# Down products of a two-layer trunk: weight remainders subtracted on the vector engine, results alternating between two PSUM rings

## The chip, the cores and the metric

The kernel runs on one core of one Trainium2 chip. The metric is the device time of one execution, in microseconds (us). The profile names the engines PE (matrix products), PEld (their weight loads), DVE (vector engine), ACT (scalar engine), POOL (general-purpose engine, here above all an issuer of DMAs) and SP (the queue that issues most loads). Each engine takes its own instructions strictly in order.

## The reference

Two layers work on 128 context tokens and 512 latent tokens of width 1024, 640 columns in all:

```python
def ffn_sublayer(x, mod, k, g, w_in, w_out):
    h = modulated_norm(x, mod, k, g)
    gt, up = jnp.split(h @ w_in, 2, axis=-1)
    return x + 0.5 * mod[:, None, 3 * k + 2] * ((jax.nn.silu(gt) * up) @ w_out)

def trunk_layer(...):
    x = ffn_sublayer(x, mod, 0, norm_g[0], w_ffn_in[0], w_ffn_out[0])
    ...
    x = ffn_sublayer(x, mod, 2, norm_g[2], w_ffn_in[1], w_ffn_out[1])
```

Between the two sublayers stands a mixer of attention, pooling and convolution heads. The change concerns the second product of each of the four feed-forward sublayers (FFNs), `@ w_out`, with 2816 inner rows and 1024 outputs. I call it the down product.

## The kernel before

**Split products.** Every float32 product is made of three products of shorter numbers (`mm3`, L352 to L354): high weights by high data, high weights by low data, low weights by high data. So each weight tile that a DMA brings into a `raw` buffer becomes a high part `wh` (a rounding copy on ACT, L170) and a low part `wl`, which is raw minus `wh`. `split_w` has two ways to make `wl`. With an engine given, that engine subtracts (L176). Without one, ACT writes `-wh` into `wl` (L173), and POOL issues a DMA that adds `raw` onto it (L174). Buffers: `raw` 5, `wh` 4, `wl` 4 tiles of 128x1024. All stages share them: the weights of the up products (`w_ffn_in`), of the down products (`w_ffn_out`), and the tiles of the modulation product (`w_ada`, loaded at L150).

**Down product.** The 22 inner tiles of 128 rows come in five chunks (`FF_CHUNKS`: 5, 5, 4, 4, 4). After the up products of a chunk, `down(ch)` runs over the eight output tiles `x0` to `x7` and, for each, over two halves of 320 columns, which I call h0 and h1. One half takes 15 products (12 with four inner tiles) into one PSUM bank of the ring `acc` (4 banks). Then `update_x` (L518) on DVE adds the bank times the gate onto `x`: in two pieces of 128 and 192 columns for h0, in one of 320 for h1. Only then is the bank free. A weight tile is 128x640 and serves one output tile in chunks 0 and 1; it is 128x1024 and serves two in chunks 2 to 4. The last chunk goes through `last_product`, with all four weight tiles made beforehand.

**What lies around it.** In FFN 1 (layer 0, first) the up products are plain, and DVE also computes a modulation product from `w_ada` tiles (L309, L311). In the other three FFNs the up products from j = 3 on use a scheme with fewer products: `fast_weights` needs sums of weight blocks on DVE (L646) and splits of them (L176). There `fast_ends` of the last j is put off until the next j, so two `acc` banks (`a` and `c`) and one `wh`/`wl` tile stay taken during a down product. A second ring `mis` (3 banks) serves the modulation product on PE (L275), transposes and norms. In FFNs 2 and 3 a running modulation step holds one of its banks for several j.

**Order.** A scheduler puts each engine's instructions in order when the program is built; it also decides which buffer a tile takes and which semaphores a load waits for. So the loads, sums and splits of the next j stand among the updates of a down product.

Of the kernel before, what the change touches and what calls it, by code (L numbers as in the profile page):

```python
# [17 lines left out]
P = 128  # L18
# [78 lines left out]
def trunk_kernel(ctx: ExitStack, tc: tile.TileContext, i: dict, o: dict):  # L97
    nc = tc.nc
# [12 lines left out]
    def acc():  # L111
        return acc_p.tile([P, 512], F32, tag="acc", name="acc")

    def mis():
        return mis_p.tile([P, 512], F32, tag="mis", name="mis")
# [4 lines left out]
    def f32(ap):  # L120
        return ap.bitcast(F32)
# [14 lines left out]
    for b in range(T // P):  # L136
        s = slot(name="xin", shape=(D,))
        src = i["x_prompt"][0] if b == 0 else i["x_sample"][0, (b - 1) * P : b * P, :]
# [19 lines left out]
    def raw_w(loads, nk=KD, width=P, raw=None):  # L158

        raw = (raw or raw_tile())[:, : nk * width].rearrange("p (k c) -> p k c", k=nk)  # L160
        loads(raw)
        return raw, nk, width

    def split_w(raw, nk, width, eng=None):

        view = lambda t: t[:, : nk * width].rearrange("p (k c) -> p k c", k=nk)
        size, tag = (1024, "") if nk * width > 512 else (512, "s")
        h = view(whp.tile([P, size], F32R, tag="wh" + tag, name="wh", bufs=4 if tag == "" else 2))
        lo = view(wlp.tile([P, size], F32R, tag="wl" + tag, name="wl", bufs=4 if tag == "" else 2))
        nc.scalar.activation(h, raw, AF.Copy)  # L170
        if eng is None:

            nc.scalar.activation(lo, f32(h), AF.Copy, scale=-1.0)  # L173
            nc.gpsimd.dma_start(lo, raw, accum_op=ALU.add)  # L174
        else:
            eng.tensor_tensor(lo, raw, f32(h), op=ALU.subtract)  # L176
        return h, lo

    def load_raw(src, c0, width=P, raw=None):
        return raw_w(  # L180
            lambda raw: nc.sync.dma_start(raw, src[:, c0 : c0 + width].rearrange("(k p) c -> p k c", p=P)),
            src.shape[0] // P,
            width,
            raw,
        )
# [1 line left out]
    def load_w(loads, nk=KD, width=P):  # L187
        return split_w(*raw_w(loads, nk, width))

    def load_cols(src, c0, width=P):  # L190
        return split_w(*load_raw(src, c0, width))

    def load_rows(n, *loads):

# [31 lines left out]
    ps = mis()  # L226
# [124 lines left out]
    def mm3(out, wh, wl, xh, xl, start, stop, onto=False):  # L351
        nc.tensor.matmul(out, wh, xh, start=start, stop=False, skip_group_check=onto)  # L352
        nc.tensor.matmul(out, wh, xl, start=False, stop=False, skip_group_check=onto)  # L353
        return nc.tensor.matmul(out, wl, xh, start=False, stop=stop, skip_group_check=onto)  # L354
# [160 lines left out]
    def update_x(l, n, t, hf, ps):  # L515
        a = HALVES[hf][0]
        for s, e, j in SEGS[hf]:
            nc.vector.scalar_tensor_tensor(  # L518
                xT[t][:, s:e],
                ps[:, s - a : e - a],  # L520
                gates[l][n][:, t, j : j + 1],
                xT[t][:, s:e],
                op0=ALU.mult,
                op1=ALU.add,
            )

    def last_product(ws, rhs, l, n, finish, nxt):

        for hf, (a, b) in enumerate(HALVES):
            for t in range(KD):  # L530
                wh, wl = ws[t // 2]
                c = slice(t % 2 * P, t % 2 * P + P)
                ps = acc()
                for k in range(4):
                    mm3(
                        ps[:, :HALF],
                        wh[:, k, c],
                        wl[:, k, c],
                        rhs[k][:, 0, a:b],
                        rhs[k][:, 1, a:b],  # L540
                        k == 0,
                        k == 3,
                    )
                update_x(l, n, t, hf, ps)
                finish(t, hf)
                nxt(hf, t)
                yield
# [8 lines left out]
    def ffn(l, f, n, hs, side, finish, nxt, first=None):  # L556
        w_in = i["w_ffn_in"][l, f]
        w_out = i["w_ffn_out"][l, f]
        gs = {}

        def weights(j, s):
            return load_cols(w_in, s * DFF + j * P)
# [55 lines left out]
        def down(ch):  # L618
            j0, j1 = FF_CHUNKS[ch]
            nj = j1 - j0  # L620
            wide = 2 if nj <= 4 else 1
            for t0 in range(0, KD, wide):
                wh, wl = load_cols(w_out[j0 * P : j1 * P, :], t0 * P, wide * P)
                for t in range(t0, t0 + wide):
                    c = slice((t - t0) * P, (t - t0 + 1) * P)
                    for hf, (a, b) in enumerate(HALVES):
                        ps = acc()
                        for j in range(nj):
                            mm3(
                                ps[:, :HALF],  # L630
                                wh[:, j, c],
                                wl[:, j, c],
                                gs[j0 + j][:, 0, a:b],
                                gs[j0 + j][:, 1, a:b],
                                j == 0,
                                j == nj - 1,
                            )
                        update_x(l, n, t, hf, ps)
# [76 lines left out]
        for j in range(2, NJ):  # L715
            if first or j < PLAIN:
                up(j)
            else:
                ends = fast_ups(j, ends)
            side(j)  # L720
            if ch < len(FF_CHUNKS) - 2 and j == FF_CHUNKS[ch][1] + (2 if first else 1):
                down(ch)
                ch += 1
        ends()
        down(ch)
        j0, j1 = FF_CHUNKS[-1]
        ws = [load_cols(w_out[j0 * P : j1 * P, :], m * 256, 256) for m in range(4)]
        for _ in last_product(ws, [gs[j] for j in range(j0, j1)], l, n, finish, nxt):
            pass

# [605 lines left out]
    for x, (l, n) in enumerate(steps):  # L1336
        last = x == len(steps) - 1
        fast = not last and steps[x + 1][1] != 1
        new = Seven() if fast else Plain()
        if last:  # L1340
            nxt = output
        else:
            heads = []

            def nxt(hf, t):
                if t < KD - 1:
                    return
                heads.append(norm_head(hf))
                if hf == 1 and fast:
                    seven(*steps[x + 1], new, heads)  # L1350
                elif hf == 1:
                    for h in range(2):
                        norm_tail(*steps[x + 1], h, new, heads[h])

        finish = nothing if last else squares
        if n == 1:
            mixer(l, hs, finish, nxt)
        else:
            ffn(l, n // 2, n, hs, spread(budget.get((l, n), 0), 1 if x else 4, x == 0), finish, nxt, None if x else first_tiles)
        hs = new  # L1360
# [30 lines left out]
```

## Time and profile before

| | |
|---|---|
| median of 3 runs | 2430.79 us (2415.92 to 2435.45) |
| profiled execution | 2416.3 us, its span 2414.5 us |
| busy share: PE, DVE, ACT, POOL | 96%, 59%, 47%, 9% |
| mean granted PE clock | 0.985 of full |

The span runs from the first to the last instruction. A PE product of 320 columns is recorded with about 0.31 us, but a new one starts every 0.15 us, since they overlap; so the busy share says little, and idle stretches and the granted clock say more. "Idle before" is time in which an engine had nothing running, with what ended it.

### The profile page before, as it was taken

The page shows a single profiled execution, that of the slowest core. Times are in us where ns is not written, and L with a number is a line of the kernel's source. Part 1 is how long each engine was busy: PE and PEld are TensorE (multiplying, and loading weights), DVE is VectorE, ACT ScalarE, POOL GpSimd, SP SyncE. Part 2 cuts the span into 40 slices and gives each one's busy share as a digit, 9 for nine tenths or more (in the row PEclk, how much of TensorE's full clock was granted, in tenths as well). Part 3 has the DMA queues.
Part 4 walks back from the last instruction along what each step waited for, and adds up shares of the span by engine and source line. Part 5 has one row for each costly group of instructions (what it writes and reads, how often), then busy time and mean ns, then how long its engine had stood idle before and what let it go on. Part 6 is the DMA issues. An engine that isn't in the chain of part 4 may idle for free.

```text
span 2414.5 us, 41180 instructions
## 1 busy us (share of the span) xinstructions
PE 2319.0 (96%) x16594; PEld 2234.9 (93%) x16594; DVE 1424.6 (59%) x3021; ACT 1146.1 (47%) x1964; POOL 221.0 (9%) x269
## 2 busy tenths in 40 slices
PE   7899999999999999999999999999999989999999
PEld 6899999999978999999999999999898789999999
DVE  5546564456867646456577364574657675546563
ACT  4433333345667434343465353444566674344451
POOL 2111111111200010100000101001111000000000
PEclk9999999999999999999999999999999999999999
DMA  8879798867633564664654545536474243543433
GB/s 268 217 167 252 189 252 197 213 133 149 140 71 95 142 157 140 159 182 123 166 140 120 134 117 147 156 108 163 107 159 112 53 97 85 130 97 99 121 100 94
DMA packets 372119, 347.22 MB, mean 144 GB/s; under 512 B 29176, under 2 KB 304984, under 8 KB 371928
## 3 DMA queue, kind: packets, MB, share of 16 engines
q1 hardware_dynamic: 340932, 244.88, 33.9%
q0 software_dynamic: 30816, 99.63, 22.7%
q8 instruction: 131, 2.15, 0.4%
q14 instruction: 60, 0.49, 0.1%
q10 hardware_dynamic: 180, 0.07, 0.0%
HBM read 242.04 MB, written 2.88 MB: 101 GB/s over the span
## 4 chain that ended last, share of the span: by engine, by line
PE 70%; issue 12%; DMA 10%; DVE 5%; ACT 2%; POOL 1%; POOLq 0%; ACTq 0%; SPq 0%; DVEq 0%
PE acc L352 21%; PE acc L353 20%; PE acc L354 20%; DMA wl<-raw 5%; DMA raw<-in_w_ffn_in 4%; PE mis L275 2%; PE po L352 1%; PE po L353 1%; PE po L354 1%; POOL wl L174 1%; DMA raw<-in_w_ada 1%; PE acc L1060 1%; PE mis L1111 1%; PE po L1100 1%; DVE sums L646 1%
## 5 line engine op out<-in xcount | busy, mean ns | idle before, releaser
L352 PE MATMUL acc<-h,wh 128*128 128x320 f32 (+1 forms) x2808 | 879.6, 315 | 27.6 <-DVE x L518 6.3
L354 PE MATMUL acc<-h,wl 128*128 128x320 f32 (+1 forms) x2808 | 870.9, 311 | 10.1 <-DMA wl<-raw 10.1
L353 PE MATMUL acc<-h,wh 128*128 128x320 f32 (+1 forms) x2808 | 873.5, 312 | 4.5 <-DVE h L412 3.9
L170 ACT ACTIVATE wh<-raw 128x1024 fp32r<-128x1024 f32 (+2 forms) x332 | 305.7, 924 | 641.2 <-PE acc L353 462.3
L352 PEld LDWEIGHTS acc<-h,wh 128*128 128x128 f32 x2808 | 531.7, 190 | 44.0 <-issue 8.0
L354 PEld LDWEIGHTS acc<-h,wl 128*128 128x128 f32 x2808 | 531.8, 190 | 13.1 <-DMA wl<-raw 12.9
L353 PEld LDWEIGHTS acc<-h,wh 128*128 128x128 f32 x2808 | 532.4, 190 | 6.7 <-DVE h L412 4.1
L352 PE MATMUL acc<-g,wh 128*128 128x320 f32 x1408 | 442.8, 314 | 29.2 <-DVE x L518 29.2
L353 PE MATMUL acc<-g,wh 128*128 128x320 f32 x1408 | 441.2, 313 | 0.0
L354 PE MATMUL acc<-g,wl 128*128 128x320 f32 x1408 | 440.3, 313 | 0.2 <-DMA wl<-raw 0.2
L174 POOL DMA_DIRECT2D wl<-raw x214 | 186.6, 872 | 2072.5 <-ACT wl L173 1409.5
L518 DVE SCALAR_TENSOR_TENSOR x<-acc,gate,x 128x128 f32<-128x128 f32 (+2 forms) x480 | 195.5, 436 | 265.3 <-PE acc L354 264.0
L352 PEld LDWEIGHTS acc<-g,wh 128*128 128x128 f32 x1408 | 269.6, 191 | 33.3 <-DVE x L518 25.8
L354 PEld LDWEIGHTS acc<-g,wl 128*128 128x128 f32 x1408 | 269.3, 191 | 0.7 <-DMA wl<-raw 0.4
L353 PEld LDWEIGHTS acc<-g,wh 128*128 128x128 f32 x1408 | 269.5, 191 | 0.3
L170 ACT ACTIVATE wh<-sums 128x1024 fp32r<-128x1024 f32 x114 | 120.5, 1059 | 203.1 <-PE acc L353 169.9
L173 ACT ACTIVATE wl<-wh 128x1024 fp32r<-128x1024 f32 (+1 forms) x214 | 205.5, 961 | 3.5
L176 DVE TENSOR_TENSOR wl<-sums,wh 128x1024 fp32r<-128x1024 f32 x114 | 139.5, 1225 | 74.0 <-ACT wh L170 54.5
L311 DVE SCALAR_TENSOR_TENSOR sums<-raw,c,sums 128x512 f32<-128x512 f32 x196 | 134.5, 746 | 37.8 <-DMA raw<-in_w_ada 37.8
L646 DVE TENSOR_TENSOR sums<-raw 128x512 f32<-128x512 f32 x114 | 74.8, 688 | 85.0 <-DMA raw<-in_w_ffn_in 84.3
L176 DVE TENSOR_TENSOR wl<-raw,wh 128x1024 fp32r<-128x1024 f32 (+1 forms) x116 | 110.9, 958 | 15.2 <-ACT wh L170 13.8
L671 ACT ACTIVATE part<-acc 128x320 f32<-128x320 f32 x171 | 73.2, 428 | 36.7 <-PE acc L354 35.1
(201 smaller groups left out, 2527.8 us busy)
## 6 DMA issues: line engine op xcount, KB each, us to landing
raw<-in_w_ffn_in SPq DMA_DIRECT2D x176, 512.0 KB, 4.2
wl<-raw POOLq DMA_DIRECT2D x150, 512.0 KB, 5.5
raw<-in_w_ada SPq DMA_DIRECT2D x128, 512.0 KB, 4.8
raw<-in_w_ffn_out SPq DMA_DIRECT2D x48, 512.0 KB, 4.8
raw<-in_w_ffn_out SPq DMA_DIRECT2D x64, 320.0 KB, 3.7
wl<-raw POOLq DMA_DIRECT2D x64, 320.0 KB, 4.4
raw<-in_w_in SPq DMA_DIRECT2D x20, 512.0 KB, 5.7
adaw<-in_w_ada SPq DMA_DIRECT2D x16, 512.0 KB, 10.6
```

Of the source, the lines that this page charges most:

```text
L170: nc.scalar.activation(h, raw, AF.Copy)
L173: nc.scalar.activation(lo, f32(h), AF.Copy, scale=-1.0)
L174: nc.gpsimd.dma_start(lo, raw, accum_op=ALU.add)
L176: eng.tensor_tensor(lo, raw, f32(h), op=ALU.subtract)
L275: last = nc.tensor.matmul(ps[32 * g : 32 * g + 32, 0:P], c2[:, 2 * q + k, :], r[:, k, g * P : (g + 1) * P], start=(q + k == 0), stop=(q + ...
L311: nc.vector.scalar_tensor_tensor(part[:, j, :], r[:, k, :], c, part[:, j, :], op0=ALU.mult, op1=ALU.add)
L352: nc.tensor.matmul(out, wh, xh, start=start, stop=False, skip_group_check=onto)
L353: nc.tensor.matmul(out, wh, xl, start=False, stop=False, skip_group_check=onto)
L354: return nc.tensor.matmul(out, wl, xh, start=False, stop=stop, skip_group_check=onto)
L518: nc.vector.scalar_tensor_tensor(xT[t][:, s:e], ps[:, s - a : e - a], gates[l][n][:, t, j : j + 1], xT[t][:, s:e], op0=ALU.mult, op1=ALU.add,)
L646: add = lambda out, x, y: nc.vector.tensor_tensor(out, x, y, op=ALU.add)
L671: nc.scalar.activation(t, ps[:, :HALF], AF.Copy)
```

## The change

Two edits, both in the down products. The weights of all down products, `last_product`'s too, now get their low part by subtraction on DVE, where ACT's negated copy and POOL's adding DMA did it before. And in `down` the bank of h1 comes from `mis`, that of h0 from `acc` as before. `last_product` keeps `acc` for both halves.

```diff
-    def load_cols(src, c0, width=P):
-        return split_w(*load_raw(src, c0, width))
+    def load_cols(src, c0, width=P, eng=None):
+        return split_w(*load_raw(src, c0, width), eng)
...
             for t0 in range(0, KD, wide):
-                wh, wl = load_cols(w_out[j0 * P : j1 * P, :], t0 * P, wide * P)
+                wh, wl = load_cols(w_out[j0 * P : j1 * P, :], t0 * P, wide * P, nc.vector)
                 for t in range(t0, t0 + wide):
                     c = slice((t - t0) * P, (t - t0 + 1) * P)
                     for hf, (a, b) in enumerate(HALVES):
-                        ps = acc()
+                        ps = (acc, mis)[hf]()
...
-        ws = [load_cols(w_out[j0 * P : j1 * P, :], m * 256, 256) for m in range(4)]
+        ws = [load_cols(w_out[j0 * P : j1 * P, :], m * 256, 256, nc.vector) for m in range(4)]
```

PE's products keep their order, but for one small one of 128 columns; they only write other banks. What moves is seen at the first down product of FFN 2. SP's queue there, before: the loads of down weights 3 to 7 (`in_w_ffn_out`), then those of the next j (`in_w_ffn_in`), with the semaphores that each waits for. DMASW stands for DMAs that POOL issued, DMAHW for those of SP.

```order
L181 DMA raw_9226<-in_w_ffn_out 128x5x128 [waits DMAHW4_49,DMASW0_49,Activation_49]
L181 DMA raw_9268<-in_w_ffn_out 128x5x128 [waits DMAHW2_49,PE_49]
L181 DMA raw_9310<-in_w_ffn_out 128x5x128 [waits DMAHW5_49,DMASW1_49,Activation_49]
L181 DMA raw_9394<-in_w_ffn_out 128x5x128 [waits DMAHW6_49,DMASW2_49,Activation_49]
L181 DMA raw_9436<-in_w_ffn_in 128x8x128 [waits DMAHW7_49,DMASW3_49,Activation_49]
L181 DMA raw_9438<-in_w_ffn_in 128x8x128 [waits DMAHW0_49,DMASW4_49,Activation_49]
```

The same loads now:

```order
L181 DMA raw_9195<-in_w_ffn_out 128x5x128 [waits DMAHW4_49,DVE_49]
L181 DMA raw_9236<-in_w_ffn_out 128x5x128 [waits DMAHW5_49,DVE_49]
L181 DMA raw_9277<-in_w_ffn_out 128x5x128 [waits DMAHW2_49,PE_49]
L181 DMA raw_9359<-in_w_ffn_out 128x5x128 [waits DMAHW6_49,DVE_49]
L181 DMA raw_9400<-in_w_ffn_in 128x8x128 [waits DMAHW7_49,DVE_49]
L181 DMA raw_9402<-in_w_ffn_in 128x8x128 [waits DMAHW0_49,DVE_49]
```

The loads stand in the same order; those that waited for the landing of an adding DMA now wait for DVE. The pair of `in_w_ffn_in` waited for the adding DMAs of down weights 3 and 4, and now waits for their subtractions.

DVE's queue at the updates of `x2` and `x3` of that down product, before:

```order
L518 SCALAR_TENSOR_TENSOR x2_94<-acc_9209,gate02_4741,x2_94 128x320
L518 SCALAR_TENSOR_TENSOR x3_95<-acc_9233,gate02_4741,x3_95 128x128
L518 SCALAR_TENSOR_TENSOR x3_95<-acc_9233,gate02_4741,x3_95 128x192
L646 TENSOR_TENSOR sums_9440<-raw_9436,raw_9438 128x512
L646 TENSOR_TENSOR sums_9440<-raw_9438 128x512
L176 TENSOR_TENSOR wl_9451<-raw_9438,wh_9450 128x512
L518 SCALAR_TENSOR_TENSOR x3_95<-acc_9251,gate02_4741,x3_95 128x320
```

And now, from the subtraction of down weight 4 on:

```order
L176 TENSOR_TENSOR wl_9239<-raw_9236,wh_9238 128x640
L518 SCALAR_TENSOR_TENSOR x2_94<-acc_9160,gate02_4721,x2_94 128x128
L518 SCALAR_TENSOR_TENSOR x2_94<-acc_9160,gate02_4721,x2_94 128x192
L518 SCALAR_TENSOR_TENSOR x2_94<-mis_9178,gate02_4721,x2_94 128x320
L646 TENSOR_TENSOR sums_9404<-raw_9400,raw_9402 128x512
L176 TENSOR_TENSOR wl_9280<-raw_9277,wh_9279 128x640
L646 TENSOR_TENSOR sums_9404<-raw_9402 128x512
L518 SCALAR_TENSOR_TENSOR x3_95<-acc_9201,gate02_4721,x3_95 128x128
L518 SCALAR_TENSOR_TENSOR x3_95<-acc_9201,gate02_4721,x3_95 128x192
```

The subtractions of the down weights stand among the updates. The first sum of the next j, which reads the pair of `in_w_ffn_in`, has moved up by one half: from behind h0 of `x3` to behind h1 of `x2`, ahead of the subtraction of down weight 5 (`wl_9280`). The same move is found in five more down products of FFNs 2 to 4, those of chunks 0 and 1; in chunk 2 the sums stand around the updates of `x0` in both kernels.

## Rows read from the trace of the kernel before

**Rows 1.** The page's first part: engine, busy us (share), instructions.

```profile
PE 2319.0 (96%) x16594; PEld 2234.9 (93%) x16594; DVE 1424.6 (59%) x3021; ACT 1146.1 (47%) x1964; POOL 221.0 (9%) x269
```

**Rows 2.** The view of waits: waiting line, releaser, total us, times, longest.

```profile
PE acc L352 <- DVE x L518: 35.6, 12, 4.6
DVE sums L646 <- DMA raw<-in_w_ffn_in: 84.3, 30, 6.2
DVE sums L311 <- DMA raw<-in_w_ada: 37.8, 12, 6.6
```

**Rows 3.** Groups by line: down products' first products; busy, mean ns, idle before.

```profile
L352 PE MATMUL acc<-g,wh 128*128 128x320 f32 x1408 | 442.8, 314 | 29.2 <-DVE x L518 29.2
```

**Rows 4.** Windows: down products of FFN 1, then nine of FFNs 2 to 4, summed.

```profile
core 0: us, PE busy (x) PEld busy (x) DVE busy (x) ACT busy (x) POOL busy (x), PEclk, DMA share, GB/s
162.10:197.70 35.60, 35.60 (x246) 35.60 (x243) 18.14 (x40) 13.92 (x19) 6.96 (x8) 1.00 0.81 193
376.20:404.50 28.30, 28.30 (x198) 28.29 (x195) 20.31 (x46) 8.65 (x11) 3.46 (x4) 1.00 0.88 223
...
862.10:903.40 41.30, 37.36 (x244) 37.00 (x242) 15.75 (x33) 10.45 (x15) 5.21 (x6) 0.96 0.69 169
...
sum 342.70, PE 313.30 PEld 310.24 DVE 145.91 ACT 88.80 POOL 36.33; mean PE 34.81 PEld 34.47 DVE 16.21 ACT 9.87 POOL 4.04
```

**Rows 5.** Timeline of PE at 886 us: start, us, engine, line, idle before.

```profile
881.89 0.31 PE L354 MATMUL acc<-g,wl 128*128 128x320 f32 x1
886.14 0.42 PE L352 MATMUL acc<-g,wh 128*128 128x320 f32 x1 [3.94 <-DVE x L518]
```

**Rows 6.** Timeline of DVE, 875 to 886 us.

```profile
875.62 0.55 DVE L518 SCALAR_TENSOR_TENSOR x<-acc,gate,x 128x320 f32<-128x320 f32 x1 [1.53 <-PE acc L354]
877.82 0.68 DVE L518 SCALAR_TENSOR_TENSOR x<-acc,gate,x 128x128 f32<-128x128 f32 x2 [1.66 <-PE acc L354]
883.72 1.29 DVE L646 TENSOR_TENSOR sums<-raw 128x512 f32<-128x512 f32 x2 [5.22 <-DMA raw<-in_w_ffn_in]
...
885.54 0.55 DVE L518 SCALAR_TENSOR_TENSOR x<-acc,gate,x 128x320 f32<-128x320 f32 x1
```

**Rows 7.** Windows after two gaps: PE's products in brackets, PEclk after POOL.

```profile
886.10:890.30 4.20, 4.16 (x18) 4.16 (x19) 2.09 (x5) 0.50 (x1) 0.85 (x1) 0.59 0.84 202
890.30:894.50 4.20, 4.20 (x30) 4.20 (x30) 1.00 (x3) 1.03 (x3) 0.86 (x1) 1.00 0.58 162
315.30:320.00 4.70, 4.70 (x19) 4.70 (x19) 4.70 (x10) 0.00 (x0) 0.44 (x1) 0.50 1.06 234
```

**Rows 8.** Timelines of SP, then the loads for the next j.

```profile
873.24 0.37 SPq L181 DMA_DIRECT2D raw<-in_w_ffn_in  x1
...
879.36 0.37 SPq L181 DMA_DIRECT2D raw<-in_w_ffn_in  x1
```

**Rows 9.** Waits of SP's queue, 860 to 885 us.

```profile
SPq L181 <- DMA wl<-raw: 16.0, 4, 5.7
```

**Rows 10.** Timelines of ACT and of POOL: down weight 4.

```profile
871.05 0.74 ACT L170 ACTIVATE wh<-raw 128x640 fp32r<-128x640 f32 x1 [2.90 <-PE acc L353]
871.82 0.74 ACT L173 ACTIVATE wl<-wh 128x640 fp32r<-128x640 f32 x1
...
872.97 0.86 POOL L174 DMA_DIRECT2D wl<-raw  x1 [3.56 <-ACT wl L173]
```

**Rows 11.** Groups by shape: subtractions on DVE; busy us, mean ns.

```profile
L176 DVE TENSOR_TENSOR wl<-raw,wh 128x1024 fp32r<-128x1024 f32 x59 | 72.1, 1223 | 13.2 <-ACT wh L170 11.7
L474 DVE TENSOR_TENSOR h<-full,h 128x640 fp32r<-128x640 f32 x36 | 28.1, 820 | 12.1 <-ACT h L473 12.1
```

**Rows 12.** Timelines of DVE and PE behind FFN 1's second down product.

```profile
313.66 0.75 DVE L311 SCALAR_TENSOR_TENSOR sums<-raw,c,sums 128x512 f32<-128x512 f32 x1 [6.59 <-DMA raw<-in_w_ada]
...
314.93 0.64 PE L352 MATMUL acc<-h,wh 128*128 128x322 f32 x1 [4.63 <-DVE x L518]
```

## The prediction

> **What bounds the kernel now.** I read the busy shares first: PE 96%, DVE 59%, ACT 47% [rows 1]. So what can be had is what PE waits for. The view of waits names one wait of the down products: PE for an update of `x`, 12 times, 35.6 us, at most 4.6 us [rows 2]. 29.2 us of it fall on the first product of a half [rows 3]: nine waits, one in each of the nine chunks 0 to 2 of FFNs 2 to 4. The other three (6.4 us) stand ahead of up products.
>
> Next the stretches. The same down product takes 35.6 us with five inner tiles and 28.3 us with four in FFN 1, where PE has no gap in it and full clock; the nine take 342.7 us together, the first 41.3 [rows 4]. At FFN 1's pace they would take 6 x 35.6 + 3 x 28.3 = 298.5 us. **The excess is 44.2 us**: 29.2 idle and 15.0 of something else. The clock is most of that: after the gap of 3.94 us [rows 5] PE is granted 0.59 of its clock, that is 1.2 GHz for most of 4.2 us, and does 18 products there, against 30 in the next 4.2 us at 2.4 GHz [rows 7]. Twelve products of 0.14 us are 1.7 us; a stall of 4 us costs nearly 6.
>
> Now one stall, backwards. PE stops behind 881.89 and goes on at 886.14, when an update frees a bank [rows 5]. DVE was through with h0 of `x3` at 878.5, then waited 5.22 us for a load of `w_ffn_in`, which its next instruction (L646) reads; h1 of `x3` came only at 885.54 [rows 6]. Two of the four `acc` banks are held by the pending `fast_ends`, so PE gets 2.2 us ahead of the updates and no further. The load was late because SP issued it late: the pair went out at 873.24 and 879.36 [rows 8], after waits for adding DMAs (16.0 us in this stretch [rows 9]). The second waited for down weight 4: rounded at 871.05 to 871.79, negated to 872.56, its adding DMA issued at 872.97 [rows 10] and, by SP's release, landed at 879.3. The cause is thus a raw buffer that stays taken 7.6 us after its rounding copy.
>
> **The change part by part.**
>
> *The release of raw.* A subtraction of 128x640 lasts 0.82 us, one of 128x1024 1.22 us [rows 11]. Down weight 4 has its `wh` at 871.79, DVE is free of h1 of `x1` at about 871.75, so the subtraction ends near 872.6 and SP can issue the second load at 872.7 instead of 879.36. With the 4.3 us that this load took (879.36 to 883.7) it lands near 877.0: 6.7 us earlier. Down weight 3 releases the first load in the same way, near 868.3 instead of 873.24.
>
> *The banks.* h1 moves to `mis`; with one bank held by a modulation step two are left, and `acc` has two. PE can now run four halves ahead instead of two: 4.4 us more.
>
> *The order on DVE.* The first sum now stands behind h1 of `x2`, done at 876.17 [rows 6]; by the times above DVE waits about 0.9 us there. PE has banks until the end of h1 of `x4`, near 884.1 at its free pace. For PE not to stop, h0 of `x3` must be updated by then, and it stands behind two sums and a subtraction (2.2 us) and needs 0.7 us itself: the load must land before 881.2. It had landed at 883.7; 877.0 leaves 4 us of room. The same reckoning holds for the other five stalls of chunks 0 and 1; in chunk 2 the sums stand at `x0`, where the load has 4 us to gain and had 2 to 4 to lose. So I take **all nine stalls away but 4 us in sum**, which I leave for the later arrivals in chunk 2: 40 us. The bounds are 44.2 (all) and 0.
>
> *DVE's new work.* 64 subtractions of 0.82 us and 48 of 1.22 us: 111 us more, and as much as that less on ACT. None is on the path if it ends before PE needs the weight. Down weight 5 is the nearest: it stands behind the first sum, ends near 878.6, and PE wants it at 884.1. DVE is busy for 16.2 us of a mean 38.1 in the nine stretches [rows 4]; eight subtractions add 6.6 us, so it keeps a third of the time free. I take nothing. If that cover is gone, a chunk of FFNs 2 to 4 costs at most its subtractions, 6.6 us, and all twelve chunks that `down` runs in FFN 2 to 4 some 70 us.
>
> The Trainium skill speaks against this direction: Perfetto Trace Analysis, section Optimizing Scalar/DVE Operations, says that work which both can do may be moved to the scalar engine where the vector engine is saturated, and here it goes the other way, onto the busier of the two. By that rule the 111 us would be on the path wherever DVE is the late engine; the trace agrees that PE waits for DVE, but shows DVE itself waiting for a load, not saturated.
>
> *ACT and POOL.* The negated copies and 112 issues of adding DMAs go. Nobody on the path waits for them save through raw, counted above. A gain from fewer bytes in flight may come on top; I take nothing.
>
> *FFN 1.* Here two waits stand ahead of up products, the larger 4.63 us [rows 12]; the clock then costs 2 more: 19 products in 4.7 us at 0.50 [rows 7], where 30 in 4.2 us would give 34. With the small third wait (in FFN 2) this makes 6.4 + 2.1 = 8.5 us. PE wanted `acc` banks that updates held, and DVE was waiting 6.59 us for a `w_ada` tile [rows 12]. Now h1 lies in `mis`, so the up products find `acc` banks free that h0 left long before; but the `w_ada` tile may be as late as ever, since DMA shares are 0.81 and 0.88 there [rows 4], and DVE gets 25 us of subtractions in this FFN (16 x 0.82 + 12 x 1.22 = 27.8, less their overlap). I take half, 4 us; the bounds are +8.5 and -25.
>
> Sum: 40 + 4 = 44 us, from 2416.3 us of the profiled execution to **2372 us**. That execution is at the low end of the runs; their median is 0.6% above it, and the same factor would give 2386. I forecast 2380, between the two.
>
> **The rivals.**
>
> *A: half of it is given back.* PE comes out of each down product 4 to 6 us earlier and needs the next j's weights then. These hang on sums and on `wh` tiles that PE itself frees, so they move along with PE, and the trace has no PE wait there today. Against me is that DVE has more in its queue by then, and the loads that follow the pair also queue in SP. A second half of 20 us gained is then 2396, by the runs' median 2408.
>
> *B: nothing moves.* The load is late for another reason than the raw buffer, say the DMA engines (a share of 0.69 in the first of the nine stretches [rows 4]), and the four banks do not suffice, since the sum has moved up by one half: 2416 to 2431.
>
> *C: slower, because DVE closes a ring.* Now the subtraction both feeds PE and frees raw, and it stands behind a sum that waits for a load, which waits for an earlier subtraction. Place: the first sum and down weight 5. If the load lands at L, PE goes on at L + 1.5, and was to start on that weight at 884.1; the stall equals today's 3.94 us when L is 886.5, that is, when the pair lands 2.8 us later than today. From there on the nine stalls are as long as before or longer, and FFN 1 carries its 25 us: 2441. For it: SP waits for DVE in FFN 1 too, and DVE waits 37.8 us for `w_ada` there [rows 2]. Against it: weights are made three tiles ahead, 13 us. The Trainium skill's rule above would lead here too.
>
> *D: the second ring is not there.* If modulation steps held two `mis` banks, PE would have three halves instead of four, 2.2 us less: still enough by the 4 us of room. No time of its own.
>
> **How the numbers follow.** Forecast 0.72, A 0.14, B 0.08, C 0.06. The range leaves out C and part of B; its low end takes 44.2 + 8.5 us and a few more for loads that get faster (2358), its high end A by the runs' median and some of B: 2418. A measurement of this kernel tells about 1% from no change, that is 24 us: faster holds the forecast and nearly half of A, 0.78; within 1% the rest of A, B and a mild C, 0.16; slower 0.06.
>
> **What would show it.** In the changed kernel's profile the row of PE's waits for `x` should fall from 35.6 us to under 8; the nine stretches should take 36 and 28 to 29 us with a clock of 1.00; the first load of a pair should be issued within 1 us of a subtraction; DVE's waits for `in_w_ffn_in` (84.3 us) should fall by 30 or more, and its busy time should rise by about 110 us, ACT's fall by about 100. I am wrong if PE waits for `wl` from DVE in the down products, if the gaps return right behind them, or if FFN 1 grows.

## The result and the profile after

The changed kernel takes **2362.39 us** (median of 4 runs, 2359.89 to 2367.3), the kernel before 2424.26 us (median of 4, one more than when the forecast was made, 2415.92 to 2435.45): a ratio of 0.9744, 95% interval [0.9694, 0.9795]. Five more runs in a later session (e8) gave 2362.37 us and 0.9758 [0.9738, 0.9779]. The profiled execution took 2359.9 us with a span of 2358.1, so 56.4 us less than the one before. The forecast was 2380 us, from a sum of 44 us.

The first part of its page answers to [rows 1], the view of waits to [rows 2] (waiting line, releaser, total us, times, longest):

```profile
PE 2302.1 (98%) x16594; PEld 2220.2 (94%) x16594; DVE 1526.2 (65%) x3133; ACT 1055.0 (45%) x1852; POOL 123.9 (5%) x157
```

```profile
PE acc L354 <- DMA wl<-raw: 10.5, 10, 1.7
...
PE mis L265 <- DVE arow L264: 2.7, 3, 1.4
...
DVE sums L646 <- DMA raw<-in_w_ffn_in: 49.4, 27, 4.9
DVE sums L311 <- DMA raw<-in_w_ada: 25.8, 10, 5.7
```

DVE does 101.6 us more and ACT 91.1 us less. PE's row for an update of `x` (35.6 us) is gone. DVE's wait for `w_ffn_in` fell by 34.9 us, that for `w_ada` by 12.0; neither is zero, they only end before PE needs a bank. The groups of the page (busy, mean ns, idle before) answer to [rows 3]: the 29.2 us are now 0.0 in either ring.

```profile
L352 PE MATMUL acc<-g,wh 128*128 128x320 f32 x832 | 258.2, 310 | 0.0
...
L352 PE MATMUL mis<-g,wh 128*128 128x320 f32 x576 | 177.8, 309 | 0.0
```

The windows of the down products, first and third of FFN 1, then the same two of FFN 2, and last the sum over the nine of FFNs 2 to 4, answer to [rows 4]:

```profile
core 0: us, PE busy (x) PEld busy (x) DVE busy (x) ACT busy (x) POOL busy (x), PEclk, DMA share, GB/s
163.70:199.20 35.50, 35.50 (x245) 35.47 (x242) 24.30 (x49) 10.46 (x13) 2.59 (x3) 1.00 0.61 164
...
369.80:398.00 28.20, 28.20 (x197) 28.16 (x194) 21.74 (x47) 7.83 (x9) 2.60 (x3) 1.00 0.70 167
857.10:892.50 35.40, 35.40 (x243) 35.40 (x241) 19.46 (x40) 6.94 (x9) 0.00 (x0) 1.00 0.45 132
...
1052.30:1080.60 28.30, 28.30 (x196) 28.27 (x193) 17.68 (x36) 4.29 (x5) 0.00 (x0) 1.00 0.40 124
...
sum 296.90, PE 296.90 PEld 296.72 DVE 177.66 ACT 58.59 POOL 0.00; mean PE 32.99 PEld 32.97 DVE 19.74 ACT 6.51 POOL 0.00
```

The nine took 342.7 us and take 296.9: **45.8 us**, all of the excess of 44.2 and a little more, since the longer ones now take 35.1 to 35.5 us where those of FFN 1 took 35.6. From the start of the first to the start of the third down product of FFN 1 it was 214.1 us and is 206.1: **8.0 us**. The other 2.6 us are a net of small waits elsewhere. The same 56 us read from PE's busy time: idle fell from 95.5 to 56.0 us, and the same 16594 products took 16.9 us less, 16.4 of them in the nine stretches, where the clock no longer falls.

The first stall of the nine, timelines of SP (two loads, from the start of the first to the end of the second), ACT and DVE (start, us, engine, line, idle before). All stands 5.0 us earlier than before, by the window's start.

```profile
863.34 4.78 SPq L181 DMA_DIRECT2D raw<-in_w_ffn_in  x2
```

```profile
866.12 0.74 ACT L170 ACTIVATE wh<-raw 128x640 fp32r<-128x640 f32 x1 [3.67 <-PE mis L353]
```

```profile
862.49 0.82 DVE L176 TENSOR_TENSOR wl<-raw,wh 128x640 fp32r<-128x640 f32 x1
...
866.90 0.82 DVE L176 TENSOR_TENSOR wl<-raw,wh 128x640 fp32r<-128x640 f32 x1
...
870.64 0.55 DVE L518 SCALAR_TENSOR_TENSOR x<-mis,gate,x 128x320 f32<-128x320 f32 x1 [1.53 <-PE mis L354]
872.62 0.69 DVE L646 TENSOR_TENSOR sums<-raw 128x512 f32<-128x512 f32 x1 [1.43 <-DMA raw<-in_w_ffn_in]
873.23 0.82 DVE L176 TENSOR_TENSOR wl<-raw,wh 128x640 fp32r<-128x640 f32 x1
...
874.56 0.67 DVE L518 SCALAR_TENSOR_TENSOR x<-acc,gate,x 128x128 f32<-128x128 f32 x2
```

The first load goes out at 863.34, right behind the subtraction of down weight 3, which ends at 863.31. Down weight 4 is rounded at 866.12 and subtracted by 867.72, and the second load is issued near 867.75; in the times of before that is 872.75, in place of 879.36 [rows 8]. The data come 4.9 us after the issue, and the sum waits 1.43 us for them where it waited 5.22 [rows 6].

### The profile page after: what moved, and what is told of

Same layout as the page of the kernel before. It is cut to its first block, busy times and chain, and to the rows that moved or that the text cites. A ratio compares the mean times of both kernels' runs of the same rounds, so it can differ in the third digit from the quotient of the medians.

```text
span 2358.1 us, 40880 instructions
## 1 busy us (share of the span) xinstructions
PE 2302.1 (98%) x16594; PEld 2220.2 (94%) x16594; DVE 1526.2 (65%) x3133; ACT 1055.0 (45%) x1852; POOL 123.9 (5%) x157
## 4 chain that ended last, share of the span: by engine, by line
PE 82%; issue 7%; DMA 5%; DVE 4%; ACT 2%; POOL 0%; SPq 0%; ACTq 0%; POOLq 0%; DVEq 0%
PE acc L352 21%; PE acc L353 21%; PE acc L354 21%; PE mis L353 3%; PE mis L352 3%; PE mis L354 3%; DMA wl<-raw 2%; PE mis L275 2%; PE po L352 1%; DMA raw<-in_w_ffn_in 1%; PE po L353 1%; PE po L354 1%; DMA raw<-in_w_ada 1%; PE acc L1060 1%; PE mis L1111 1%
## 5 line engine op out<-in xcount | busy, mean ns | idle before, releaser
L354 PE MATMUL acc<-h,wl 128*128 128x320 f32 (+1 forms) x2808 | 870.7, 311 | 10.5 <-DMA wl<-raw 10.5
L176 DVE TENSOR_TENSOR wl<-raw,wh 128x1024 fp32r<-128x1024 f32 (+2 forms) x228 | 222.2, 975 | 58.9 <-ACT wh L170 54.5
L352 PE MATMUL acc<-g,wh 128*128 128x320 f32 x832 | 258.2, 310 | 0.0
L353 PE MATMUL acc<-g,wh 128*128 128x320 f32 x832 | 258.0, 310 | 0.0
L354 PE MATMUL acc<-g,wl 128*128 128x320 f32 x832 | 257.3, 309 | 0.0
L174 POOL DMA_DIRECT2D wl<-raw x102 | 89.5, 877 | 1734.2 <-DVE x L518 967.8
L518 DVE SCALAR_TENSOR_TENSOR x<-acc,gate,x 128x128 f32<-128x128 f32 (+1 forms) x352 | 125.2, 394 | 84.5 <-PE acc L354 82.8
L353 PE MATMUL mis<-g,wh 128*128 128x320 f32 x576 | 177.9, 309 | 0.0
L354 PE MATMUL mis<-g,wl 128*128 128x320 f32 x576 | 177.8, 309 | 0.0
L352 PE MATMUL mis<-g,wh 128*128 128x320 f32 x576 | 177.8, 309 | 0.0
L352 PEld LDWEIGHTS acc<-g,wh 128*128 128x128 f32 x832 | 156.3, 188 | 1.8 <-issue 1.6
L354 PEld LDWEIGHTS acc<-g,wl 128*128 128x128 f32 x832 | 156.4, 188 | 0.2
L353 PEld LDWEIGHTS acc<-g,wh 128*128 128x128 f32 x832 | 156.3, 188 | 0.3
L311 DVE SCALAR_TENSOR_TENSOR sums<-raw,c,sums 128x512 f32<-128x512 f32 x196 | 135.2, 745 | 26.1 <-DMA raw<-in_w_ada 25.8
```

The source lines that it names most:

```text
L311: nc.vector.scalar_tensor_tensor(part[:, j, :], r[:, k, :], c, part[:, j, :], op0=ALU.mult, op1=ALU.add)
L518: nc.vector.scalar_tensor_tensor(xT[t][:, s:e], ps[:, s - a : e - a], gates[l][n][:, t, j : j + 1], xT[t][:, s:e], op0=ALU.mult, op1=ALU.add,)
```

## The experiments

Ratios are to the kernel before, run on the same chip in the same session.

| run | edit | median us | ratio [95%] |
|---|---|---|---|
| e1_sub_only | subtraction, one ring | 2366.65 | 0.9756 [0.9743, 0.9769] |
| e2_banks_only | two rings, adding DMA | 2383.22 | 0.9822 [0.98, 0.9844] |
| e3_sub_twice | the change, each subtraction done twice | 2368.25 | 0.9764 [0.975, 0.9779] |
| e4_ffn1_old | the change, not in FFN 1 | 2378.15 | 0.9802 [0.9788, 0.9815] |
| e5_before_raw6 | before, one more raw buffer | 2406.6 | 0.9942 [0.9921, 0.9963] |
| e6_pool_sub | the change, subtraction on POOL | 2360.31 | 0.9749 [0.9727, 0.977] |
| e7_plain_sub | the change, plain up weights subtracted too | 2359.82 | 0.9747 [0.9726, 0.9768] |
| e8_change_again | the changed kernel | 2362.37 | 0.9758 [0.9738, 0.9779] |
| e9_order_only | before, sums placed later | 2384.48 | 0.9845 [0.981, 0.9881] |
| e10_pool_plain | e6 and e7 together | 2360.07 | 0.9743 [0.9706, 0.9781] |
| e11_sub_at_old_place | e1, sums at the place of before | 2368.89 | 0.9775 [0.9751, 0.9799] |

**The two edits apart.** e1 undoes the second edit of the changed kernel, e2 the first.

```diff
-                        ps = (acc, mis)[hf]()
+                        ps = acc()
```

> Only the subtraction on DVE; h0 and h1 both in acc. The scheduler puts the first sum behind h1 of x2, as in the changed kernel, so the sum's place comes with the subtraction and not with the banks. My reckoning: the load lands 6.7 us earlier, but with two free acc banks PE has 2.2 us, and h0 of x3 is updated about 0.9 us after PE wants its bank; so nine short stalls of about 1 us without a fall of the clock, 9 us in all, and in FFN 1 some 3 of its 8.5 us stay: profiled execution near 2372 us. Rival (the late release is the whole cause): as the changed kernel, 2360. Rival (the banks are the whole cause): the nine stalls stay at 2 to 4 us, 2400 or more.

The reckoning of nine short stalls fell, and the time is the rival's: the release alone gives the whole gain. That it is the whole cause does not follow, since e2 and e9 take most of the stalls away without it. One gap of 0.67 us is left, in chunk 2 of FFN 2. The views of waits and DVE's timeline at the first of the nine:

```profile
PE acc L352 <- DVE x L518: 0.7, 1, 0.7
...
DVE sums L646 <- DMA raw<-in_w_ffn_in: 47.1, 27, 4.5
```

```profile
871.25 0.55 DVE L518 SCALAR_TENSOR_TENSOR x<-acc,gate,x 128x320 f32<-128x320 f32 x1 [1.53 <-PE acc L354]
872.41 0.69 DVE L646 TENSOR_TENSOR sums<-raw 128x512 f32<-128x512 f32 x1 [0.61 <-DMA raw<-in_w_ffn_in]
...
874.36 0.67 DVE L518 SCALAR_TENSOR_TENSOR x<-acc,gate,x 128x128 f32<-128x128 f32 x2
```

The sum waits 0.61 us, h0 of `x3` is updated by 875.03, and PE does not stop in this stretch. In FFN 1 no stall for an update is left either. Beside e8 the second ring is worth nothing that can be measured (0.9756 against 0.9758).

```diff
-                wh, wl = load_cols(..., t0 * P, wide * P, nc.vector)
+                wh, wl = load_cols(..., t0 * P, wide * P)
```

> Only the second ring; low parts by ACT and the adding DMA of POOL, DVE's order as before. My reckoning: the load lands as late as before (DVE still waits about 5 us at the sum, behind h0 of x3), but h1 of x3, updated at 886.1 in the times of before, frees a bank that PE wants at 886.3 only; so the nine stalls go without any earlier load, and FFN 1's too: near 2364 us, with DVE's waits for w_ffn_in loads still near 84 us. Rival (release is the whole cause): stalls shorter by at most 4.4 us each but the clock still falls, 2385 to 2400.

Two rings without the release missed that reckoning by 19 us, since another wait took a part of the old one's place. They still bring 1.8%, where the change brings 2.4 to 2.6%: PE's waits for an update fall from 35.6 to 4.3 us though the load is as late as before, and those for `wl` are 21.7 us, where the change has 10.5. Its views of waits, and timelines of ACT, POOL and PE:

```profile
PE acc L354 <- DMA wl<-raw: 21.7, 15, 3.3
...
PE acc L352 <- DVE x L518: 4.3, 2, 3.7
...
DVE sums L646 <- DMA raw<-in_w_ffn_in: 92.1, 30, 8.1
```

```profile
880.64 1.26 ACT L170 ACTIVATE wh<-raw 128x512 fp32r<-128x512 f32 x2 [6.87 <-DMA raw<-in_w_ffn_in]
881.94 0.74 ACT L173 ACTIVATE wl<-wh 128x640 fp32r<-128x640 f32 x1
```

```profile
883.08 0.87 POOL L174 DMA_DIRECT2D wl<-raw  x1 [8.02 <-ACT wl L173]
```

```profile
889.20 0.63 PE L354 MATMUL acc<-g,wl 128*128 128x320 f32 x1 [3.30 <-DMA wl<-raw]
```

The late load stops a second engine. ACT's rounding of `w_ffn_in` stands ahead of a down weight's negated copy, waits 6.87 us for the same load, and that weight's `wl` is then late by way of POOL. With two banks PE had stood still before it could see this.

**DVE's added work, and FFN 1.** e3 issues every subtraction of the change a second time, with the same result; e4 leaves FFN 1 as it was.

```diff
             eng.tensor_tensor(lo, raw, f32(h), op=ALU.subtract)
+            if again:
+                eng.tensor_tensor(lo, raw, f32(h), op=ALU.subtract)
```

> The changed kernel with each of the 112 subtractions issued twice into the same wl: about 100 to 110 us more of busy DVE, nothing else. My reckoning: down product 0 of FFN 2 has 3.9 us of room at h0 of x3 and each doubled subtraction takes 0.73 to 1.1 us of it, so the nine stay free of stalls; FFN 1 may lose a few us: +0 to +6 us against the changed kernel (2360 to 2366). Rival C (DVE closes a ring, or DVE is near its limit): 40 to 110 us more.

The first part of its page, and PE's wait for a row of the modulation step (L264 in the other kernels):

```profile
PE 2309.0 (97%) x16594; PEld 2227.8 (94%) x16594; DVE 1623.2 (68%) x3245; ACT 1055.2 (44%) x1852; POOL 124.6 (5%) x157
```

```profile
PE mis L267 <- DVE arow L266: 4.4, 3, 3.0
```

97 us more on DVE leave the ratio within the interval of the change's own (0.9764 against 0.9758; some 6 us by the medians, the upper end of the reckoning). One wait of 2.98 us shows, in FFN 1 (0.86 in the changed kernel), and in the nine stretches PE waits for no update and no subtraction: the cover is there.

```diff
-                wh, wl = load_cols(..., t0 * P, wide * P, nc.vector)
+                wh, wl = load_cols(..., t0 * P, wide * P, None if first else nc.vector)
...
-                        ps = (acc, mis)[hf]()
+                        ps = acc() if first else (acc, mis)[hf]()
```

> Both edits undone in FFN 1 only. My reckoning: the two waits of FFN 1 (1.1 and 4.6 us) and the low clock behind the second come back, 8.4 us: 2368 us, all of it before 330 us of the span. Rival: FFN 1 is bound elsewhere and the time moves to a later wait, 2360.

The stall of [rows 12] is back; view of waits:

```profile
PE acc L352 <- DVE x L518: 5.1, 2, 4.4
```

By the ratios e4 is some 11 us slower than the change. Its third down product starts at 377.3 us, that of the change at 369.8, which is 7.5 us; the rest lies in waits of the mixer and of later up products, which vary between kernels that do not differ there. FFN 1's share is thus about 8 us. In e1 and e2 no stall of that size is left there, so either edit alone removes it.

**More raw buffers instead.** e5 is the kernel before with `raw` 6 in place of 5 (and one tile less in another pool).

```diff
-    rawp = pool("raw", 5)
+    rawp = pool("raw", 6)
```

> The kernel before, with six raw buffers instead of five (paid for with 21 instead of 22 tiles in the pool slots); neither edit of the change. Theory 1 (the raw buffer is taken too long, so another buffer cures it): the load for the next j is issued 4.4 us earlier, DVE's wait of about 5 us falls to about 1 us and the nine stalls go: near 2375 us. Theory 2 (the scheduler places the first sum where it believes the load has landed, and it believes too early of whatever hangs on an adding DMA): with six buffers it has put the sum 4.4 us earlier too, behind h0 of x2 instead of x3, so DVE waits as long as before and the nine stalls stay: within 10 us of 2416. I hold theory 2.

```profile
PE acc L352 <- DVE x L518: 35.4, 14, 5.4
...
DVE sums L646 <- DMA raw<-in_w_ffn_in: 65.3, 23, 6.6
```

With a buffer more the loads go out earlier, and yet the six stalls of chunks 0 and 1 stayed (3.4 to 5.4 us). The order shows why: the scheduler moved the first sum up too, from behind h0 of `x3` to behind h0 of `x2`, where it waits 5.17 us in the first stretch. The 14 us that e5 gains by its ratio lie elsewhere, in part in chunk 2, where such waits fall from 8.4 to 3.7 us. So the place of the sum needs testing by itself.

**Place and release apart.** e9 is the kernel before with neither edit; in the down products of FFNs 2 to 4 the next j's sums are held behind h1 of `x4`, and the roundings of `w_ffn_in` behind the last down weight's. e11 has the release (e1), with the first sum held behind h0 of `x3`, where the kernel before has it.

```diff
+                        if (t, hf) == (4, 1) and not first:
+                            behind.append(last.ins)
+            if not first:
+                behind.append(rounded[0].ins)
...
+            with ExitStack() as stack:
+                while behind:
+                    stack.enter_context(tc.issue_after(behind.pop()))
+                return fast_weights_now(j)
```

> The kernel before with neither edit: the low parts of the down weights still come from the adding DMA, both halves still use the first ring, and the loads are issued in the same order and wait for the same landings. Only the place of the next j's sums and splits is moved by hand in the down products of FFNs 2 to 4: on DVE behind the update of h1 of x4 (it was h0 of x3 in chunks 0 and 1, x0 in chunk 2), on ACT behind the rounding copy of the last down weight. Theory (the stall is a matter of place: the first sum stands in the queue ahead of its load's landing, and updates behind it): the load still lands near 883.7 in the first of the nine stretches, but no update of x2 to x4 stands behind it, so the waits for the update of x in the nine stretches fall from 29.2 us to under 5, and the time from 2424 by 35 to 45 us to 2380 to 2390; the two stalls of FFN 1 (6 us idle) stay. Rival (the earlier release itself is needed): the load that comes 6.7 us later than in the changed kernel is then missed at the end of the down product, by the next j's weights; PE waits there for wl from the splits of the sums, 2 us or more in most of the nine, and the time stays above 2400.

Its view of waits, its timelines of SP and of DVE (L520 is the update, L660 the sums):

```profile
PE acc L356 <- DMA wl<-raw: 12.1, 10, 2.4
PE acc L354 <- DVE x L520: 10.7, 6, 3.3
...
DVE sums L660 <- DMA raw<-in_w_ffn_in: 55.0, 23, 5.9
```

```profile
878.19 6.28 SPq L183 DMA_DIRECT2D raw<-in_w_ffn_in  x2
```

```profile
883.21 0.68 DVE L520 SCALAR_TENSOR_TENSOR x<-acc,gate,x 128x128 f32<-128x128 f32 x2 [1.66 <-PE acc L356]
...
889.83 0.55 DVE L520 SCALAR_TENSOR_TENSOR x<-acc,gate,x 128x320 f32<-128x320 f32 x1 [1.53 <-PE acc L356]
890.29 1.28 DVE L660 TENSOR_TENSOR sums<-raw 128x512 f32<-128x512 f32 x2
```

The second load still goes out late, near 884.1 in this kernel's times, which run some 5 us behind those of before (879.36, [rows 8]), but no update stands behind its sum: the updates run on and the sum finds its data. The stalls in mid-product are gone; the time is as the theory had it, and the rival's 2400 fell. The waits left are somewhat more than the 5 us of the theory: 3.33 and 2.60 us for an update at the end of the first two products of FFN 2, where the sums of the second pair of loads now stand. Another 3.9 us are in FFN 1, which this edit leaves alone.

```diff
+                        if (t, hf) == (3, 0) and ch < 2 and not first:
+                            behind.append(last.ins)
```

> Subtraction alone (one ring, as in the run with the subtraction only), with the first sums of the next j put back by hand where the kernel before has them in chunks 0 and 1 of FFNs 2 to 4: behind h0 of x3. So the release of raw is early and the place is the old one. Theory (the stall needs both, a place ahead of the landing and a late load; either remedy alone suffices): the load lands before the sum's turn, DVE's waits for w_ffn_in in front of these sums fall away (in the sum over the kernel from 47 to about 40 us), no wait of PE for the update of x above 1 us, and the ratio is that of the subtraction alone, 0.972 to 0.980. Rival (the moved place did the work, and the earlier release only because the scheduler moved the sum for it): the stalls of chunks 0 and 1 come back, six of 3 us and more, and the ratio is 0.985 or above.

```profile
PE acc L354 <- DVE x L520: 0.7, 1, 0.7
```

```profile
875.52 0.68 DVE L520 SCALAR_TENSOR_TENSOR x<-acc,gate,x 128x128 f32<-128x128 f32 x2 [0.71 <-PE acc L356]
876.12 1.28 DVE L658 TENSOR_TENSOR sums<-raw 128x512 f32<-128x512 f32 x2
```

At the old place, with the release, the sum does not wait at all, and the time agrees with that of the subtraction alone (0.9775 and 0.9756, with intervals that overlap). The stall needs three things together: the early place, the late load and, by e2, only two free banks. Taking away any one of them is enough for most of it.

**Towards a better version.** e6 lets POOL subtract; e7 gives the plain up weights of FFNs 2 to 4 a subtraction on DVE as well; e8 is the changed kernel beside them; e10 joins e6 and e7.

```diff
-                wh, wl = load_cols(..., t0 * P, wide * P, nc.vector)
+                wh, wl = load_cols(..., t0 * P, wide * P, nc.gpsimd)
```

> The changed kernel with the 112 subtractions on POOL instead of DVE. A product of 128x512 on POOL took 1.30 us in the trace of before, so by length about 1.6 us for 128x640 and 2.6 us for 128x1024; raw is freed 0.8 to 1.4 us later than in the changed kernel, and weights are still made three tiles ahead. My reckoning: no stall in the nine, DVE busy about 110 us less, 2358 to 2370 us. Rival (DVE's sums and subtractions and POOL's slow each other): DVE's subtraction of 128x1024 rises well above 1.22 us and the time by 10 to 30 us.

```diff
-            return load_cols(w_in, s * DFF + j * P)
+            return load_cols(w_in, s * DFF + j * P, P, None if first else nc.vector)
```

> The changed kernel with the low parts of the plain up weights of FFNs 2 to 4 (three j of two tiles each) also subtracted on DVE. In the changed kernel PE still waits for adding DMAs there: six gaps of 0.5 to 1.7 us at 757, 760, 1227, 1238, 1909 and 1912 us, 6.6 us in sum. My reckoning: most of them go, 3 to 6 us less than the changed kernel. Rival (DVE is late at the start of an FFN, where it also makes the modulated inputs): 0 to 5 us more.

> The changed kernel once more, to be compared with the kernels beside it and with the one that subtracts but keeps one ring. If the second ring is worth nothing, its ratio to before lies within 0.3% of that kernel's 0.9756; if it is worth the 9 us that I reckoned, at 0.972 or less.

> The changed kernel with the down weights' subtractions on POOL in place of DVE, and in addition the plain up weights of FFNs 2 to 4 subtracted on DVE in place of the adding DMA: a sum of the two variants that each came out 2 us under the changed kernel in their sessions (not told apart from no change). If the two savings are real and add, 2356 to 2359; if they were noise, 2360 to 2364. Under both, PE waits for no update of x in the down products of FFNs 2 to 4 (under 1 us in sum).

Groups by shape in e6 (busy, mean ns, idle before), then e7's waits:

```profile
L176 POOL TENSOR_TENSOR wl<-raw,wh 128x1024 fp32r<-128x1024 f32 x50 | 119.9, 2400 | 607.7 <-ACT wh L170 518.9 <-DVE part L683 88.8
L176 POOL TENSOR_TENSOR wl<-raw,wh 128x640 fp32r<-128x640 f32 x64 | 101.1, 1580 | 562.4 <-ACT wh L170 562.4
L176 DVE TENSOR_TENSOR wl<-raw,wh 128x1024 fp32r<-128x1024 f32 x59 | 72.1, 1223 | 13.1 <-ACT wh L170 11.6
```

```profile
PE acc L352 <- ACT sg L580: 6.8, 3, 3.1
...
PE acc L354 <- DMA wl<-raw: 3.3, 3, 1.7
```

POOL takes twice as long for a subtraction, and that is still short enough: no stall for an update in the nine stretches, and the time is the change's, though DVE is held up by it (last section). In e7 PE's waits for `wl` fall from 10.5 to 3.3 us, and waits for the sigmoid (L580) come in their place. All four kernels lie within 0.9743 to 0.9758 with intervals that overlap: none is shown to be better than the change, and e10's 2360.07 us is what was reckoned for the case that both savings are noise.

## Why the prediction was right, and where its terms were off

**The stall and its release: right.** The chain was read backwards from PE's gap to a raw buffer held for an adding DMA, and its times came out nearly as worked out: first load issued at 868.34 in the times of before (863.34 and 5.0; forecast 868.3), second near 872.75 (872.7), data at 877.6 (877.0), DVE's wait at the sum 1.43 us (0.9).

**The nine stalls, forecast 40 of 44.2 us: too small.** They gave 45.8 us. The 4 us that I left for late arrivals in chunk 2 were not there; all three of chunk 2's windows take 28.3 us at full clock.

**FFN 1, forecast 4 of 8.5 us: too small.** It gave 8.0 us. I feared that the `w_ada` tile would be as late as ever; it was not (25.8 us of waits instead of 37.8), and of the 25 us of subtractions that I feared there, 0.86 us are seen as a wait of PE for the modulation row, which the kernel before and e6 do not have at that place. Together these two terms are 10 of the 12 us between the sum and the profiled execution. The 8 us that I added for the median of the runs were not needed either: those of the changed kernel lie within 0.3%.

**DVE's new work, forecast nothing: right,** and shown by doubling it (e3). By that the rule of the Trainium skill that spoke against the change (Perfetto Trace Analysis, Optimizing Scalar/DVE Operations: move work off a saturated vector engine) did not apply: a DVE that waits for a load is not short of time.

**The banks: the step that failed.** "PE can now run four halves ahead instead of two" is true, but I counted it as part of the remedy, with 4 us of room. By e1 the release needs no such room (0.9756 with one ring, 0.9758 with two). By e2 the banks are a second remedy and not a part of this one: alone they bring 1.8%, and what they leave over is in part a wait moved from DVE to ACT, which I had not looked at. Rival D, which has no time of its own, would by e1 have cost nothing.

**The moved sum: half seen.** I read from the order that the sum moved up, and reckoned that it did no harm. I didn't ask whether the place of the sum was itself the cause. e9 shows that with loads as late as before, the place alone (of the sums, and with them of ACT's roundings) brings 1.55% of the change's 2.4 to 2.6%. Why the scheduler put the sum ahead of the landing is only argued: in the change, in e1 and in e5 it moves the sum up as raw comes free earlier, and in e2, where raw does not, it leaves it; in the kernel before it had put it where the load was still 5 us away, as if it took the load to land sooner than it did.

**The rivals.** A (half given back): no PE wait followed the down products. B and C: the row of waits for `x` is gone, no subtraction made PE wait in the nine stretches. Of the forecast's signs all held: row under 8 us (gone), first load within 1 us of a subtraction (0.03 us in the stretch shown), windows of 36 and 28 to 29 us at a clock of 1.00 (35.4 and 28.3), `w_ffn_in` waits down by 30 or more (34.9), DVE up by about 110 (101.6), ACT down by about 100 (91.1).

**What stays open.** The 2.6 us that lie in neither term, and some 10 us by which profiles of nearly equal kernels differ in the mixer and at the start of FFN 4; these waits varied from kernel to kernel with no edit near them.

## What to carry to other kernels

When an engine waits for a load in the middle of a queue, ask two things: why the load is late, and why the waiting instruction stands there; either answer may be the cheap remedy, while one more buffer left most of the stalls here (e5), and more banks took most of them away but brought the next engine's wait into view (e2). A buffer's release counts from its last reader's end: here a copy, an issue and an adding DMA held it for 7.6 us, where a subtraction of 0.8 us did on an engine that had a third of its time free. Price a stall of PE with the clock behind it (here 16.9 us beside 39.5 us of idle), and expect all of it back when the gap goes.

## What the hardware showed beside this

The clock did not follow from the length of the gap alone. Windows of e9 behind its gaps of 3.33 us (906.36) and 2.60 us (1014.20), PEclk after POOL:

```profile
core 0: us, PE busy (x) PEld busy (x) DVE busy (x) ACT busy (x) POOL busy (x), PEclk, DMA share, GB/s
906.40:910.60 4.20, 4.20 (x29) 4.20 (x30) 3.83 (x6) 1.02 (x2) 0.00 (x0) 1.00 0.00 0
1014.20:1018.40 4.20, 4.20 (x19) 4.20 (x20) 3.42 (x5) 0.44 (x1) 0.00 (x0) 0.63 0.01 4
```

After the longer gap PE kept full clock (2.4 GHz) and did 29 products; after the shorter one it was granted 0.63, that is 1.2 GHz for much of the stretch, and did 19. Ahead of the first PE had no other gap over 0.15 us for 40 us, ahead of the second one of 0.97 us, 7 us earlier.

POOL's subtractions (1.58 and 2.40 us) left those of DVE as they were: 128x1024 took 1223 ns in e6 and in the change alike. They held up other work of DVE. Of the 114 operations `g<-part,g` of e6, 15 began inside a subtraction of POOL; each of them ended 0.3 to 0.4 us after it, having taken 1.48 to 2.49 us, where the other 99 took 0.49. The timelines of POOL and DVE show one of them; then come the groups in e6 and in the change.

```profile
949.13 1.58 POOL L176 TENSOR_TENSOR wl<-raw,wh 128x640 fp32r<-128x640 f32 x1 [70.12 <-ACT wh L170]
```

```profile
949.51 1.55 DVE L156 TENSOR_TENSOR g<-part,g 128x320 fp32r<-128x320 f32 x1 [0.54 <-ACT g L155]
```

```profile
L156 DVE TENSOR_TENSOR g<-part,g 128x320 fp32r<-128x320 f32 x114 | 79.5, 697 | 33.7 <-ACT g L155 33.4
```

```profile
L156 DVE TENSOR_TENSOR g<-part,g 128x320 fp32r<-128x320 f32 x114 | 55.7, 489 | 22.8 <-ACT g L155 22.6
```

The Trainium skill (Perfetto Trace Analysis, Optimizing Scalar/DVE Operations) warns that work moved between these two might not help, since they share a read port. The trace agrees in that DVE was held up; the time did not change (0.9749 in e6, 0.9758 in e8).
